# Feed forwards' inner units in three parts, one pool of 4 KB buffers, and an order of issue by traced durations

## The chip, the cores and the metric

The kernel runs on one core of a Trainium2 chip. The metric is device time in microseconds (us) of one launch, lower is better; times before are of three runs, and one more execution was profiled.

## What is computed

Two streams of 256 tokens and 1024 channels, latents (L) and context (C), pass through two layers; only the latents are returned. Shortened from the reference:

```
def ada_in(h, g, m, j):      # norm, scale, shift
    return rms_norm(h, g) * (1 + m[:, j, 1]) + m[:, j, 0]
def gated_residual(h, m, j, y, w):
    return h + w * m[:, j, 2] * y
def swiglu(x, w_in, w_out):  # 1024 -> 2 x 2816 -> 1024
    a, b = split(x @ w_in, 2); return (silu(a) * b) @ w_out

for i in range(2):           # m = silu(c) @ w_mod[i] + b_mod[i], for L and for C
    h = gated_residual(h, m, 0, swiglu(ada_in(h, g[i,0], m, 0), ...), 0.5)   # both streams
    y = retention(...) if i == 0 else neighbourhood_attention(...)
    h = gated_residual(h, m, 1, y, 1.0)
    h = gated_residual(h, m, 2, swiglu(ada_in(h, g[i,2], m, 2), ...), 0.5)
return rms_norm(h[L], final_norm_g)
```

The four feed forwards are called FFN 0 to FFN 3 here; retention stands between FFN 0 and FFN 1, attention between FFN 2 and FFN 3. Since the context isn't returned, FFN 3 and the attention's output are of the latents alone. Everything is in float32.

## The kernel before

Activations lie with channels on the 128 partitions: a stream is 8 chunks of 128 channels x 256 tokens. A product in float32 is made of three matmuls in the fp32r format: each operand is split into a high part (a cast on ScalarE, ACT) and a low part (the difference, on VectorE, DVE), and TensorE (PE) adds high x high, high x low and low x high in one bank. So each weight is loaded (`raw`), cast (`whi`) and subtracted (`wlo`) before PE can use it, and each activation too (`slot` tiles).

A feed forward (`ffn`, line 725) takes the 2816 inner units as 22 blocks of 128, in two halves of 11 (`HALF`). In each half it makes 11 gated blocks (one 1 MB weight each, two banks, 48 matmuls of both streams' 512 columns), and then adds their products with the output weights to the 8 output blocks of 128 channels: for each block n one weight of 11 x 128 columns, 33 matmuls into one bank, and one `residual` per stream, `h<-one,gate,h` on DVE. In the second half the last two output blocks (n = 6, 7) are done stream by stream: first L's two, 256 columns wide, then C's two, so that L's norm can begin while PE works on C. This norm is a chain: square (ACT), sum (DVE), sum over partitions (`rstd_rows`, two small matmuls on PE, `one<-con,t` 128x2), reciprocal root (`rsqrt`, eight small steps on DVE, `few`), diagonal (`t<-con,few`), spread over the partitions (`rstd_cols`, two matmuls `one<-t,con` 128x128), and for each of 8 chunks a scaling (`t<-h,scl,one`, DVE), a high part (ACT) and a low part (`slot<-t,modT,slot`, DVE). The next stage's first weights then run stream by stream: `pair` matmuls of 256 columns for L, later for C.

PE, DVE, ACT and GpSimd run their instructions in the order in which the program issues them; no scheduler moves them. The program sets this order by a clock of its own: each issue adds a cost to the engine's time (`account`, line 131; `Engine`, line 143; `mm`, line 258), and after each matmul `advance` (line 228) issues those steps whose time has come: norm steps (`later`), casts and subtractions of weights (`soon`), and steps of the modulation (`bg`, `acc<-mraw`: the sums of silu(c) with w_mod, one step every `BG_EVERY` us). SyncE (SP) issues the loads. Weights have buffers of their own: two `raw` of 8 KB a partition, three pairs `whi`, `wlo` of 8 KB; activations have 24 `slot` buffers of 4 KB. The costs are

```
V = Engine("dve", nc.vector, 0.06, 960.0)      # fixed us, elements per us
A_ = Engine("act", nc.scalar, 0.09, 1200.0)
account("pe", [lhsT, rhs], [out], n / 2400.0 * (1 if rhs.dtype == F32R and n >= 256 else 4) + 0.0025)
BG_EVERY = 2.2
RAWS, SPLITS = 2, 3
```

Of the kernel before, what the change touches and what calls it, by code (L numbers as in the profile page):

```python
# [17 lines left out]
P = 128  # L18
# [6 lines left out]
HALF = NHC // 2  # L25
# [4 lines left out]
H_RET = 4  # L30
BIG = 1e30

# [39 lines left out]
def trunk(ctx, tc, a):  # L72
# [4 lines left out]
    slots = ctx.enter_context(tc.tile_pool(name="slots", bufs=24))  # L77
# [83 lines left out]
    V = Engine("dve", nc.vector, 0.06, 960.0)  # L161
    A_ = Engine("act", nc.scalar, 0.09, 1200.0)
# [26 lines left out]

    plan = []  # L190

    def plan_all():
        for f in range(2):
            for hf in range(2):
                plan.extend(a["win"][f, hf * HALF + t] for t in range(HALF))
                plan.extend(a["wout"][f, hf, n] for n in range(KC))
            if f == 0:
                for hd in range(H_RET):
                    plan.extend([a["rq"][hd], a["rk"][hd], a["rv"][hd, 0], a["rv"][hd, 1]])
                    if hd:  # L200
                        plan.extend([a["ro"][hd - 1, 0], a["ro"][hd - 1, 1]])
                    plan.extend([a["rg"][hd, 0], a["rg"][hd, 1]])
                plan.extend([a["ro"][H_RET - 1, 0], a["ro"][H_RET - 1, 1]])
        for f in range(2, 4):
            for hf in range(2):
                plan.extend(a["win"][f, hf * HALF + t] for t in range(HALF))
                plan.extend(a["wout"][f, hf, n] for n in range(KC))
            if f == 2:
                for g in range(4):
                    plan.extend([a["nq"][g], a["nk"][g], a["nv"][g]])  # L210
                plan.extend(a["no"][n] for n in range(4))

    plan_all()
    RAWS, SPLITS = 2, 3
    raws, split_tiles = [], []
    state = {"loaded": 0, "freed": 0, "split": 0, "retired": 0, "bg_at": 0.0, "hold": True, "sums": True, "inside": True, "lag": (0.0, 0.0), "tight": False}
# [11 lines left out]
    def advance():  # L228
# [4 lines left out]
        while soon and not state["tight"] and soon[0][0] <= now["pe"] and ready_at(soon[0][5]) <= now["pe"] + 0.3 and free("dve", 0.5):  # L233
            soon.pop(0)[2]()
# [34 lines left out]
    def load():  # L269
# [5 lines left out]
        raws.append((t, src.shape))  # L275

    def prep():
        raw, shape = raws.pop(0)
        tile_no = state["split"]
        state["split"] += 1  # L280
        w = shape[1] * shape[2]
# [1290 lines left out]
```

## Time and profile before

| | |
|---|---|
| median of 3 runs | 1951.44 us (1949.91 to 1952.09) |
| profiled execution | 1952.25 us, span from first to last instruction 1950.2 us |
| PE busy | 1924.2 us (99%) |
| DVE busy | 1352.0 us (69%) |
| ACT busy | 687.9 us (35%) |
| loaded | 276.11 MB, 142 GB/s over the span |

Stages, in us of the span: start and FFN 0 to about 413, retention to 834, FFN 1 to 1192, FFN 2 to 1553, attention to 1746, FFN 3 and the end to 1950. "Busy" counts the time in which at least one instruction of the engine is under way; PE's matmuls overlap, so a stretch in which PE is busy throughout is one in which it never waited long enough to run empty.

### The profile page before, as it was taken

The page shows a single profiled execution, that of the slowest core. Times are in us where ns is not written, and L with a number is a line of the kernel's source. Part 1 is how long each engine was busy: PE and PEld are TensorE (multiplying, and loading weights), DVE is VectorE, ACT ScalarE, POOL GpSimd, SP SyncE. Part 2 cuts the span into 40 slices and gives each one's busy share as a digit, 9 for nine tenths or more (in the row PEclk, how much of TensorE's full clock was granted, in tenths as well). Part 3 has the DMA queues.
Part 4 walks back from the last instruction along what each step waited for, and adds up shares of the span by engine and source line. Part 5 has one row for each costly group of instructions (what it writes and reads, how often), then busy time and mean ns, then how long its engine had stood idle before and what let it go on. Part 6 is the DMA issues. An engine that isn't in the chain of part 4 may idle for free.

```text
span 1950.2 us, 26148 instructions
## 1 busy us (share of the span) xinstructions
PE 1924.2 (99%) x10458; PEld 1661.8 (85%) x10458; DVE 1352.0 (69%) x2402; ACT 687.9 (35%) x1035; POOL 73.0 (4%) x108
## 2 busy tenths in 40 slices
PE   7999999999999999999999999999999999999998
PEld 4888888898888888888888889888888899989998
DVE  5576666678788888876666676767632588887665
ACT  5422232333323232342222223322222366665443
POOL 1000000010000000100000000000000101100000
PEclk8999999999999999999999999999999999999999
DMA  7334534434434434234353343555433345544553
GB/s 287 141 137 129 187 130 136 156 119 151 142 133 141 147 130 142 86 130 149 125 179 132 140 139 98 194 189 200 162 101 82 110 119 113 98 115 167 194 176 114
DMA packets 70090, 278.85 MB, mean 143 GB/s; under 512 B 23632, under 2 KB 23888, under 8 KB 52304
## 3 DMA queue, kind: packets, MB, share of 16 engines
q1 hardware_dynamic: 69968, 277.18, 43.5%
q8 instruction: 82, 1.34, 0.3%
q14 instruction: 40, 0.33, 0.0%
HBM read 276.11 MB, written 1.05 MB: 142 GB/s over the span
## 4 chain that ended last, share of the span: by engine, by line
PE 94%; DVE 3%; ACT 2%; DMA 1%; issue 0%; SPq 0%; DVEq 0%; ACTq 0%
PE pair L259 61%; PE one L259 32%; DVE slot L151 1%; PE one L265 1%; DMA slot<-in_wmod 1%; DVE t L151 1%; ACT slot L151 1%; DVE wlo L151 1%; ACT whi L151 1%; DVE few L151 0%; DMA raw<-in_nv 0%; ACT t L151 0%; DVE h L151 0%; PE pair L265 0%; SPq L166 0%
## 5 line engine op out<-in xcount | busy, mean ns | idle before, releaser
L259 PE MATMUL pair<-slot,whi 128*128 128x512 f32 (+2 forms) x4000 | 1039.1, 351 | 6.8 <-ACT slot L151 4.7
L259 PEld LDWEIGHTS pair<-slot,whi 128*128 128x128 f32 x4000 | 696.4, 190 | 104.3 <-ACT slot L151 5.4
L259 PE MATMUL pair<-slot,wlo 128*128 128x512 f32 (+2 forms) x2000 | 682.5, 350 | 0.1
L259 PE MATMUL one<-slot,whi 128*128 128x512 f32 (+1 forms) x1860 | 481.4, 347 | 0.0
L151 DVE TENSOR_TENSOR wlo<-raw,whi 128x1024 fp32r<-128x1024 f32 (+1 forms) x400 | 436.4, 1122 | 38.5 <-ACT whi L151 37.7
L151 ACT CAST whi<-raw 128x1024 fp32r<-128x1024 f32 (+1 forms) x400 | 365.0, 959 | 225.3 <-PE one L259 138.6
L259 PEld LDWEIGHTS pair<-slot,wlo 128*128 128x128 f32 x2000 | 372.9, 190 | 48.8 <-DVE wlo L151 0.4
L259 PEld LDWEIGHTS one<-slot,whi 128*128 128x128 f32 x1860 | 325.9, 189 | 43.4
L259 PE MATMUL one<-slot,wlo 128*128 128x512 f32 (+1 forms) x930 | 323.1, 347 | 0.0
L151 DVE SCALAR_TENSOR_TENSOR acc<-mraw,sT,acc 128x512 f32<-128x512 f32 x392 | 279.2, 750 | 17.1 <-DMA mraw<-in_wmod 15.9
L151 ACT ACTIVATE t<-pair 128x512 f32<-128x512 f32 x66 | 39.4, 597 | 442.9 <-PE pair L259 442.9
L259 PEld LDWEIGHTS one<-slot,wlo 128*128 128x128 f32 x930 | 176.1, 189 | 21.8
L151 DVE TENSOR_TENSOR t<-pair,t 128x512 f32<-128x512 f32 x66 | 45.6, 692 | 204.2 <-ACT t L151 204.2
L151 DVE TENSOR_TENSOR slot<-t,slot 128x512 fp32r<-128x512 f32 (+2 forms) x144 | 88.1, 612 | 64.8 <-ACT slot L151 63.4
L151 ACT CAST slot<-t 128x512 fp32r<-128x512 f32 (+2 forms) x144 | 79.4, 552 | 122.1 <-DVE t L151 121.7
L151 DVE SCALAR_TENSOR_TENSOR h<-one,gate,h 128x256 f32<-128x256 f32 x112 | 49.6, 479 | 103.6 <-PE one L259 103.4
L151 POOL TENSOR_TENSOR t<-t,t 128x256 f32<-128x256 f32 x47 | 39.4, 850 | 1708.4 <-ACT t L151 1286.9
L259 PE MATMUL pair<-whi,slot 128*128 128x512 f32 (+1 forms) x384 | 98.5, 339 | 0.0
L259 PE MATMUL one<-slot,slot 128*128 128x512 f32 (+1 forms) x432 | 89.8, 348 | 1.3 <-DVE slot L151 1.0
L151 ACT ACTIVATE t<-h 128x256 f32<-128x256 f32 (+1 forms) x88 | 36.9, 434 | 142.8 <-DVE h L151 129.3
L259 PEld LDWEIGHTS one<-slot,slot 128*128 128x128 f32 x432 | 69.9, 189 | 10.8 <-DVE slot L151 1.4
L259 PEld LDWEIGHTS pair<-whi,slot 128*128 128x128 f32 x384 | 67.2, 189 | 7.5
(100 smaller groups left out, 1077.8 us busy)
## 6 DMA issues: line engine op xcount, KB each, us to landing
raw<-in_win SPq DMA_DIRECT2D x88, 1024.0 KB, 4.9
mraw<-in_wmod SPq DMA_DIRECT2D x128, 512.0 KB, 4.7
raw<-in_wout SPq DMA_DIRECT2D x64, 704.0 KB, 4.2
slot<-in_wmod SPq DMA_DIRECT2D x16, 512.0 KB, 10.3
raw<-in_rv SPq DMA_DIRECT2D x8, 1024.0 KB, 4.8
raw<-in_rg SPq DMA_DIRECT2D x8, 1024.0 KB, 4.9
raw<-in_ro SPq DMA_DIRECT2D x8, 1024.0 KB, 4.9
slot<-in_ex SPq DMA_DIRECT2D x8, 512.0 KB, 6.0
```

What stands on the lines that cost most here:

```text
L151: getattr(self.real, op)(*args, **kw)
L259: nc.tensor.matmul(out, lhsT=lhsT, rhs=rhs, start=start, stop=stop)
L265: nc.tensor.transpose(out=out, in_=in_, identity=ident)
```

## The change

Parts: the 22 blocks of inner units are taken in three parts of 8, 7 and 7, not in two halves of 11. So there are 96 output weights of 8 or 7 blocks instead of 64 of 11, every output block is added to `h` three times, and the last two output blocks, done stream by stream, have 7 inner blocks.

Buffers: `raw`, `whi`, `wlo` and the activations share one pool of 40 buffers of 4 KB; at most 4 hold raw weights and 12 split parts. A 1 MB weight is loaded as two halves of 512 KB.

Costs of the program's own clock: DVE and ACT get larger fixed costs, each matmul 0.0136 us on top of its columns; a background step comes every 1.6 us; `mod_sum` is held back while the values are projected; `mcol` makes the modulation's blocks that are missing.

Code for a product with 7 instead of 8 multiplications is there too (`Seven`, `seven`, `low_by_dma`), and isn't reached with `STANDARD = (22, 22, 22)`; but `operands`, which makes its inputs, is called in the third part of FFN 0, 1 and 2, and what it makes is used by nothing.

```diff
-HALF = NHC // 2
+PARTS = ((0, 8), (8, 15), (15, 22))
+SLOTS, RAWS, SPLITS = 40, 4, 12
+STANDARD, AMONG = (22, 22, 22), (2, 3, 3)
...
-    slots = ctx.enter_context(tc.tile_pool(name="slots", bufs=24))
+    slots = ctx.enter_context(tc.tile_pool(name="slots", bufs=SLOTS))
...
-    V = Engine("dve", nc.vector, 0.06, 960.0)
-    A_ = Engine("act", nc.scalar, 0.09, 1200.0)
+    V = Engine("dve", nc.vector, 0.157, 960.0)
+    A_ = Engine("act", nc.scalar, 0.155, 1150.0)
...
-        while soon and not state["tight"] and soon[0][0] <= now["pe"] and ready_at(soon[0][5]) <= now["pe"] + 0.3 and free("dve", 0.5):
+        while soon and not state["tight"] and soon[0][0] <= now["pe"] and ready_at(soon[0][5]) <= now["pe"] + 0.3 and free("dve", 0.5) and state["parts"] + soon[0][6] <= SPLITS:
...
-        account("pe", [lhsT, rhs], [out], n / 2400.0 * (1 if rhs.dtype == F32R and n >= 256 else 4) + 0.0025)
+        account("pe", [lhsT, rhs], [out], n / 2400.0 * (1 if rhs.dtype == F32R and n >= 256 else 4) + 0.0136)
...
+        for i, (raw, src) in enumerate(zip(units, srcs)):
+            n = src.shape[1] * src.shape[2]
+            hi, lo = part_tile(), part_tile()
+            def first(hi=hi, raw=raw, n=n):
+                A_.copy(out=hi[:, :n], in_=raw[:, :n])
+            def second(hi=hi, lo=lo, raw=raw, n=n):
+                V.tensor_tensor(out=lo[:, :n], in0=raw[:, :n], in1=hi[:, :n].bitcast(F32), op=ALU.subtract)
+                landed(1)
...
-    BG_EVERY = 2.2
+    BG_EVERY = 1.6
...
-        for hf in range(2):
+        for hf, (t0, t1) in enumerate(PARTS):
             gts = []
+            size, final = t1 - t0, hf == len(PARTS) - 1
...
+            if not raw and t1 == standard:
+                made_operands = operands(xt)
...
-            last = KC - 2 if hf == 1 and len(streams) == 2 else KC
+            last = KC - 2 if final and len(streams) == 2 else KC
             for n in range(2, last):
                 w, ps = weight(), one()
-                acc3(ps[:, every], terms(w, every, range(HALF)))
+                acc3(ps[:, every], terms(w, every, range(size)))
...
-                        acc3(ps[:, xc], terms(w, xc, range(HALF)))
+                        acc3(ps[:, xc], terms(w, xc, range(size)))
```

What this does to the order of issue, at three places. In the rows, the left side of the arrow is what is written; `h0` is the latents' state and `h1` the context's, `x2` means two instructions that read alike.

First, PE at the end of FFN 0, where retention begins. Before, the two spread matmuls (`one_441`) stand among the 33 matmuls of the context's last output block (`one_432`), with 29 of these behind them:

```order
L259 MATMUL one_432_3095<-slot_267_1838,whi_408_2893 128x256 x2
L259 MATMUL one_432_3095<-slot_267_1838,wlo_409_2894 128x256
L259 MATMUL one_432_3095<-slot_277_1910,whi_408_2893 128x256
L259 MATMUL one_441_3108<-t256_428_3071,con_78 128x128 x2
L259 MATMUL one_432_3095<-slot_277_1910,whi_408_2893 128x256
L259 MATMUL one_432_3095<-slot_277_1910,wlo_409_2894 128x256
L259 MATMUL one_432_3095<-slot_286_1991,whi_408_2893 128x256 x2
```

So PE had the rest of the context's block to do while DVE began the norm steps.

After, they (`one_586`) stand behind all of the context's last block (`one_562`), and the next stage's first pair (`pair_576`) directly behind them:

```order
L281 MATMUL one_562_3314<-slot_488_2885,wp_515_3047 128x256
L281 MATMUL one_562_3314<-slot_500_2970,wp_514_3046 128x256 x2
L281 MATMUL one_562_3314<-slot_500_2970,wp_515_3047 128x256
L281 MATMUL one_586_3374<-t256_566_3330,con_78 128x128 x2
L281 MATMUL pair_576_3364<-slot_578_3366,wp_531_3130 128x256
L281 MATMUL pair_576_3364<-slot_579_3367,wp_531_3130 128x256
L281 MATMUL pair_576_3364<-slot_578_3366,wp_532_3131 128x256
```

So nothing of the context stands between the spread and the pair. The row sums moved as well, from behind 17 context matmuls to behind 23 of them.

Second, DVE at the same place, from the diagonal on. Before, the context's last residual (`h1_85<-one_432`) comes amid the norm steps:

```order
L151 TENSOR_SCALAR t256_428_3071<-con_78,few_426_3061 128x128 x2
L151 SCALAR_TENSOR_TENSOR h1_85<-one_424_3039,gate_221_1443,h1_85 128x256
L151 SCALAR_TENSOR_TENSOR scl_442_3111<-modT_83,vec_80 128x8
L151 SCALAR_TENSOR_TENSOR t256_443_3116<-h0_84,scl_442_3111,one_441_3108 128x256
L151 SCALAR_TENSOR_TENSOR t256_444_3119<-h0_84,scl_442_3111,one_441_3108 128x256
L151 SCALAR_TENSOR_TENSOR slot_434_3101<-t256_443_3116,modT_83,slot_433_3100 128x256
L151 SCALAR_TENSOR_TENSOR t256_445_3133<-h0_84,scl_442_3111,one_441_3108 128x256
L151 SCALAR_TENSOR_TENSOR slot_434_3101<-t256_444_3119,modT_83,slot_433_3100 128x256
L151 SCALAR_TENSOR_TENSOR t256_446_3143<-h0_84,scl_442_3111,one_441_3108 128x256
L151 SCALAR_TENSOR_TENSOR slot_436_3103<-t256_445_3133,modT_83,slot_435_3102 128x256
L151 SCALAR_TENSOR_TENSOR h1_85<-one_432_3095,gate_221_1443,h1_85 128x256
```

Six norm steps stood ahead of that residual.

After, it and the sum of the context's squares stand between the diagonal and the first norm step:

```order
L161 TENSOR_SCALAR t256_566_3330<-con_78,few_564_3320 128x128 x2
L161 SCALAR_TENSOR_TENSOR h1_85<-one_562_3314,gate_233_1270,h1_85 128x256
L161 TENSOR_TENSOR t256_513_3041<-t256_571_3358,t256_513_3041 128x256
L161 SCALAR_TENSOR_TENSOR scl_587_3378<-modT_83,vec_80 128x8
L161 SCALAR_TENSOR_TENSOR t256_588_3380<-h0_84,scl_587_3378,one_586_3374 128x256
L161 SCALAR_TENSOR_TENSOR t256_589_3383<-h0_84,scl_587_3378,one_586_3374 128x256
L161 SCALAR_TENSOR_TENSOR slot_579_3367<-t256_588_3380,modT_83,slot_578_3366 128x256
```

The first norm step (`t256_588`) moved behind two steps that wait for the context's end.

At the ends of FFN 1 and FFN 2 the two orders differ in the same way, with one of the unused subtractions and two of weights' in the stretch besides.

Third, DVE where FFN 1 begins, in the context's norm. Before, two subtractions of weights (`wlo`) stand between the diagonal and the first norm step:

```order
L151 TENSOR_SCALAR t256_971_6679<-con_78,few_969_6669 128x128 x2
L151 TENSOR_TENSOR wlo_946_6522<-raw_883_6127,whi_945_6521 128x1024
L151 SCALAR_TENSOR_TENSOR scl_973_6706<-modT_83,vec_80 128x8
L151 TENSOR_TENSOR wlo_946_6522<-raw_883_6127,whi_945_6521 128x1024
L151 SCALAR_TENSOR_TENSOR t256_975_6723<-h1_85,scl_973_6706,one_972_6703 128x256
L151 SCALAR_TENSOR_TENSOR t256_976_6729<-h1_85,scl_973_6706,one_972_6703 128x256
L151 SCALAR_TENSOR_TENSOR slot_934_6490<-t256_975_6723,modT_83,slot_933_6489 128x256
L151 SCALAR_TENSOR_TENSOR t256_977_6741<-h1_85,scl_973_6706,one_972_6703 128x256
L151 SCALAR_TENSOR_TENSOR slot_934_6490<-t256_976_6729,modT_83,slot_933_6489 128x256
```

From the first norm step on nothing came between the steps for a while.

After, two stand ahead of the small steps, and two more (`wp`, as these parts are named now) between the first low part and the third scaling:

```order
L161 TENSOR_SCALAR t256_1196_7012<-con_78,few_1194_7002 128x128 x2
L161 SCALAR_TENSOR_TENSOR scl_1198_7044<-modT_83,vec_80 128x8
L161 SCALAR_TENSOR_TENSOR t256_1199_7049<-h1_85,scl_1198_7044,one_1197_7041 128x256
L161 SCALAR_TENSOR_TENSOR t256_1200_7052<-h1_85,scl_1198_7044,one_1197_7041 128x256
L161 SCALAR_TENSOR_TENSOR slot_1153_6801<-t256_1199_7049,modT_83,slot_1152_6800 128x256
L161 TENSOR_TENSOR wp_1179_6906<-raw_1127_6621,wp_1178_6905 128x1024
L161 TENSOR_TENSOR wp_1181_6908<-raw_1128_6623,wp_1180_6907 128x1024
L161 SCALAR_TENSOR_TENSOR t256_1203_7086<-h1_85,scl_1198_7044,one_1197_7041 128x256
L161 SCALAR_TENSOR_TENSOR slot_1153_6801<-t256_1200_7052,modT_83,slot_1152_6800 128x256
L161 SCALAR_TENSOR_TENSOR t256_1204_7092<-h1_85,scl_1198_7044,one_1197_7041 128x256
L161 SCALAR_TENSOR_TENSOR slot_1155_6803<-t256_1203_7086,modT_83,slot_1154_6802 128x256
```

So the second low part (`slot_1153` from `t256_1200`) moved behind two subtractions.

## Rows read from the trace of the kernel before

**Rows 1.** The page, busy time of each engine, share of the span, instructions.

```profile
PE 1924.2 (99%) x10458; PEld 1661.8 (85%) x10458; DVE 1352.0 (69%) x2402; ACT 687.9 (35%) x1035; POOL 73.0 (4%) x108
```

**Rows 2.** Windows: length; busy time (instructions) of PE, PEld, DVE, ACT, POOL; granted clock; DMA.

```profile
413.70:800.00 386.30, 386.30 (x1859) 325.69 (x1858) 318.86 (x581) 123.20 (x157) 0.00 (x0) 1.00 0.41 138
1727.00:1755.00 28.00, 24.02 (x183) 22.17 (x182) 23.43 (x61) 17.80 (x40) 1.62 (x2) 1.00 0.34 114
```

**Rows 3.** Groups of instructions by form: count, busy us, mean ns of one, idle before.

```profile
L151 DVE TENSOR_TENSOR wlo<-raw,whi 128x1024 fp32r<-128x1024 f32 x272 | 324.3, 1222 | 21.5 <-ACT whi L151 21.0
...
L151 DVE TENSOR_TENSOR slot<-t,slot 128x512 fp32r<-128x512 f32 x98 | 67.8, 692 | 56.8 <-ACT slot L151 56.3
...
L151 DVE SCALAR_TENSOR_TENSOR h<-one,gate,h 128x256 f32<-128x256 f32 x112 | 49.6, 479 | 103.6 <-PE one L259 103.4
```

**Rows 4.** Timeline of PE, FFN 0 to retention: start, us, line, operation.

```profile
404.70 0.40 PE L259 MATMUL one<-slot,whi 128*128 128x256 f32 x2
...
406.74 0.51 PE L259 MATMUL one<-con,t 128*128 128x2 f32 x4
...
409.58 0.60 PE L259 MATMUL one<-t,con 128*128 128x128 f32 x4
...
413.49 0.40 PE L259 MATMUL pair<-slot,whi 128*128 128x256 f32 x2
...
419.69 1.36 PE L259 MATMUL pair<-slot,whi 128*128 128x256 f32 x10
```

**Rows 5.** Timeline of DVE, the same stretch.

```profile
404.90 0.48 DVE L151 SCALAR_TENSOR_TENSOR h<-one,gate,h 128x256 f32<-128x256 f32 x1 [2.34 <-PE one L259]
...
407.28 0.16 DVE L151 TENSOR_SCALAR few<-one 128x2 int32<-128x2 int32 x1 [0.86 <-PE one L259]
...
409.30 0.48 DVE L151 SCALAR_TENSOR_TENSOR h<-one,gate,h 128x256 f32<-128x256 f32 x1
...
410.22 0.87 DVE L151 SCALAR_TENSOR_TENSOR t<-h,scl,one 128x256 f32<-128x256 f32 x2 [0.36 <-PE one L259]
411.28 0.48 DVE L151 SCALAR_TENSOR_TENSOR slot<-t,modT,slot 128x256 fp32r<-128x256 f32 x1 [0.19 <-ACT slot L151]
...
413.70 0.49 DVE L151 SCALAR_TENSOR_TENSOR h<-one,gate,h 128x256 f32<-128x256 f32 x1 [0.35 <-PE one L259]
...
414.88 0.42 DVE L151 TENSOR_TENSOR t<-t,t 128x256 f32<-128x256 f32 x1
...
417.85 0.48 DVE L151 SCALAR_TENSOR_TENSOR slot<-t,modT,slot 128x256 fp32r<-128x256 f32 x1 [0.18 <-ACT slot L151]
```

**Rows 6.** Timeline of PE, retention to FFN 1.

```profile
833.84 0.60 PE L259 MATMUL one<-t,con 128*128 128x128 f32 x4
...
838.83 0.40 PE L259 MATMUL pair<-slot,whi 128*128 128x256 f32 x2
```

**Rows 7.** Timeline of PE, end of the attention; in brackets the idle time before.

```profile
1735.75 0.63 PE L265 MATMUL one<-con,t 128*128 128x128 f32 x4 [0.52 <-DVE t L151]
...
1737.06 0.74 PE L259 MATMUL one<-slot,slot 128*128 128x256 f32 x4 [0.32 <-ACT slot L151]
1738.32 0.74 PE L259 MATMUL one<-slot,slot 128*128 128x256 f32 x4 [0.52 <-DVE slot L151]
...
1741.81 0.84 PE L259 MATMUL pair<-slot,whi 128*128 128x256 f32 x2 [1.33 <-ACT slot L151]
```

**Rows 8.** The page, DMA issues: count, KB each, us from issue to landing.

```profile
mraw<-in_wmod SPq DMA_DIRECT2D x128, 512.0 KB, 4.7
```

**Rows 9.** Windows of the start, columns as in rows 2.

```profile
24.00:28.00 4.00, 2.33 (x11) 1.67 (x12) 3.45 (x11) 2.53 (x6) 0.00 (x0) 0.92 1.01 406
28.00:30.00 2.00, 1.93 (x9) 1.64 (x9) 2.00 (x4) 2.00 (x4) 0.00 (x0) 0.50 1.02 408
38.00:40.00 2.00, 1.29 (x4) 1.06 (x5) 1.82 (x6) 1.31 (x3) 0.00 (x0) 0.50 0.05 18
44.00:46.00 2.00, 2.00 (x12) 1.91 (x11) 2.00 (x3) 2.00 (x3) 0.00 (x0) 0.50 0.00 0
```

More of the change, by code (lines that the diff above doesn't have):

```diff
@@ L213, in trunk @@
     plan_all()
-    RAWS, SPLITS = 2, 3
-    raws, split_tiles = [], []
-    state = {"loaded": 0, "freed": 0, "split": 0, "retired": 0, "bg_at": 0.0, "hold": True, "sums": True, "inside": True, "lag": (0.0, 0.0), "tight": False}
+    raws, split_tiles, active = [], [], []
+    state = {"loaded": 0, "raw": 0, "split": 0, "parts": 0, "limit": SPLITS, "bg_at": 0.0, "hold": True, "sums": True, "inside": True, "lag": (0.0, 0.0), "tight": False}
     soon = []
@@ L300, in pump, with released @@
+    def released(n):
+        state["parts"] -= n
+        pump()
     def pump():
         while True:
-            if raws and state["split"] - state["retired"] < SPLITS:
+            if raws and (not split_tiles if raws[0][0] == "seven" else
+                         state["parts"] + 2 * len(raws[0][1]) <= state["limit"] and not any(x[6] for x in soon)):
                 prep()
-            elif state["loaded"] < len(plan) and state["loaded"] - state["freed"] < RAWS:
+            elif state["loaded"] < len(plan) and state["raw"] + len(plan[state["loaded"]][1]) <= RAWS:
@@ L446, in mcol @@
         c0 = (j * 3 + w) * KC
-        assert all((l, v, (c0 + k) // 4) in made for k in range(kk.start, kk.stop))
+        while not all((l, v, (c0 + k) // 4) in made for k in range(kk.start, kk.stop)):
+            if due:
+                mod_sum(*due.pop(0)[1])
+            else:
+                next(bg, None)
         return modT[:, l, v, c0 + kk.start:c0 + kk.stop]
@@ L782, in ffn @@
                 state["hold"] = False
-            for t in range(len(gts), HALF):
+            for t in range(len(gts), size):
+                if t0 + t == standard:
+                    x7 = made_operands()
+                    state["limit"] = SPLITS
+                if in_seven(2 * l + which, t0 + t):
+                    gts.append(slot([P, 2, 512], F32R))
+                    seven(t, gts[t], x7)
+                    continue
+                if not raw and t0 + t == standard - 3 and standard < PARTS[0][1]:
+                    made_operands = operands(xt)
+                if t0 + t == standard - 3 and standard == PARTS[0][1]:
+                    state["limit"] = SPLITS - 4
                 wh, wl = weight()
```

288 lines of the change are left out of this document (231 added, 57 removed).

## The prediction, made before the changed kernel ran

> **What bounds the kernel now.** I read the page's table of engines first: TensorE (PE) is busy 1924.2 of 1950.2 us, VectorE (DVE) 1352.0 [rows 1]. A PE row counts as busy while its pipeline drains, so 99% does not say that PE runs at its peak; but it says that PE hardly ever waits. The windows say where it does: not at all from 413.70 to 800.00, which is all of retention but its end, and 3.98 us (28.00 - 24.02) at the end of the attention [rows 2]. The remaining idle PE time is the start and the last 8 us, which the change leaves as they are (the first 130 instructions of PE's order read the same in both kernels).
>
> So two things can move the time: the number and width of the matmuls, and new waits of PE. Everything that DVE and ACT do is free until PE arrives at an instruction whose operand isn't there. The places where this is decided are those where one stage's output must pass a chain of small steps before the next stage's first matmul: residual, square, sum, reciprocal root, spread over the columns, scaled and split.
>
> That chain as it runs now, from FFN 0 to retention: PE has finished the latents' last two output blocks and starts on the context's at 404.70. DVE adds the last residual (404.90), ACT squares, PE sums rows at 406.74, eight small steps and the diagonal run on DVE from 407.28 to 409.30, PE spreads the result at 409.58, the first norm step is at 410.22, the last low part is written from 417.85 to 418.33 [rows 4, 5]. Beside it PE does 66 context matmuls of 256 columns. Their pitch is 0.120 us (seventeen stand ahead of the row sums, from 404.70 to 406.74), so they are 7.92 us of cover. PE starts the next stage's first pair at 413.49, and 404.70 + 7.92 + 0.37 (rows) + 0.36 (spread) = 413.35: no wait. The low part of the eighth chunk is ready at 418.33, and PE asks for it at about 413.49 + 42 x 0.120 = 418.5 or a little after. So this chain fits with next to nothing to spare.
>
> **The change part by part.**
>
> *Matmuls.* The last two output blocks are done stream by stream in 256 columns, and now have 7 inner units instead of 11. By the two orders there are 144 matmuls of 256 columns less and 72 of 512 columns more. At 0.120 us for the narrow ones, and between 0.213 (512 columns at the granted 2.4 GHz; the clock is 1.00 in [rows 2]) and 0.240 (twice a narrow one) for the wide ones, this is -1.9 to 0 us. I take **-0.9**.
>
> *Cover of the three chains: FFN 0 to retention, FFN 1 to FFN 2, FFN 2 to attention.* The same 7 for 11 takes the context's cover from 66 to 42 matmuls, 5.04 us. The order shows two things more: the row sums now stand 23 matmuls behind the latents' end (before: 17), and on DVE the last context residual and its sum stand ahead of the first norm step, not amid the norm steps. Counted from the context's first matmul, after, by the durations of before:
> - row sums at 23 x 0.120 = 2.76; small steps 0.54 behind them (406.74 to 407.28), but not before the first context residual, so 3.4; diagonal done 2.02 later (407.28 to 409.30), 5.4;
> - the last context matmul ends its issue at 5.04 + 0.37 = 5.41, so its residual starts at about 5.65, and its sum 1.18 later (413.70 to 414.88), 6.83; the first norm step behind both, 7.25 (before: 410.22 - 404.70 = 5.52);
> - from the first norm step to the end of the last low part it takes 418.33 - 410.22 = 8.11 now, with a residual and a sum amid it that use up 0.40 and 0.34; without them 7.37. So the last low part is there at 14.6;
> - PE needs it some 0.7 us before the end of the first weight's latent part: 15.3. Before, this end was at 419.69 - 404.70 = 15.0, with 24 x 0.120 = 2.88 us more work in it.
>
> The loss is 15.3 - (15.0 - 2.88) = 3.2 us for each, **+9.6** for three. Bounds: if the residual and its sum do not delay the first norm step, it is 7.25 - 5.52 = 1.7 less each (1.5, in all 4.5); if the weights' subtractions, 1.22 us [rows 3], that stand in the chain at the second and third place are in the way once each, 12.0.
>
> *Retention to FFN 1.* The cover is the same, but DVE's order is not. Now the spread stands at 833.84 and the context's first pair at 838.83 [rows 6], 5.0 us. After, only 13 matmuls (1.56 us) stand between spread and pair, and two subtractions stand behind the first low part. From the spread to the first low part it takes 2.18 us (409.58 to 411.28 + 0.48 [rows 4, 5]), so PE, which comes 1.56 + 0.36 behind it, waits 0.3. The second low part comes two subtractions (2.3), a norm step and itself (0.4 + 0.4) later, at 5.3; PE wants it 12 matmuls after the first, at 3.7: 1.6 more. With some 0.4 for a later spread, **+2.3** (0 if the subtractions were done early, 3 if all of it shows).
>
> *End of the attention.* The four waits ahead of the last head's products and its share of the output projection sum to 0.52 + 0.32 + 0.52 + 1.33 = 2.69 us [rows 7]. In the order of after 18 + 24 = 42 projection matmuls stand between that head's last product and the first matmul that needs its result, not 12. That is 30 x 0.120 = 3.6 us of cover more, which takes the wait of 1.33 away and may take part of the others: **-2.0** (0 to -2.7).
>
> *Costed at nothing.* (a) 56 more residuals of 0.479 us are 26.8 us of DVE; the unused operands that are still built after each of the first three feed forwards are 24 sums of 128x512 (0.692 each) and 24 operations of 128x1024 (1.222 each), 46 us of DVE [rows 3], and 12 casts on ACT. DVE is idle for 598 us [rows 1] and PE goes ahead meanwhile; if this cover were gone in the 386 us stretch, where DVE is at 318.86 [rows 2], there would be 67 us left. Only the steps within the chains above count, and they are in the sums. (b) The pieces in which weights are loaded are half as large, and PE's first use of one stands at least 26 us of matmuls behind its load in the order, where the least was 12; a load of that size lands in 4.7 us [rows 8]. (c) The background steps come every 1.6 us, not 2.2, but they are as many: they are done earlier, out of retention and FFN 2 into the stages before.
>
> *Sum:* 9.6 + 2.3 - 0.9 - 2.0 = +9.0. The profiled execution took 1952.25 us, 0.8 over the median of 1951.44. So 1960.4 against the median, **1960.5**.
>
> **The rivals.**
>
> *The clock falls too.* A wait of 3 us may cost more than itself. At the start, PE was busy only 2.33 of 4.00 us from 24 to 28, and its granted clock was 0.50 (1.2 GHz) in the next 2 us; after a second thin stretch it was at 0.50 from 38 to 46, though PE was busy all of the last 2 us ([rows 9]; of the four rows from 38 to 46, which all have 0.50, the first and the last stand there). It did not fall at the attention's end, where the idle time came in pieces of at most 1.33 us (clock 1.00 [rows 2]). At half clock a stretch of 3 to 8 us loses 1.5 to 4 us, for each of three waits: +5 to +12 if all fall, so **1967** (1964 to 1973). For it: the wait of about 3 us in one piece. Against it: the four waits of the attention's end, which followed closely, did not do it. [...]
>
> *The waits close up (no change).* The chain runs tighter because nothing interrupts it, and the first norm step comes at 5.5, not 7.25; the weights' subtractions are done ahead. Then 4.5 + 0 - 0.9 - 2.0 = +1.6, or +0.9 with the attention's end in full: **1952.5**. For it: DVE still idles 0.36, 0.19 and 0.35 us between steps of the chain [rows 5], which could close. Against it: the residual follows PE's end within 0.2 us (413.49 to 413.70 [rows 4, 5]) and can't come sooner, and in the new order all of the chain stands behind it.
>
> *The new order wins.* One mechanism: the three chains stay covered, because the row sums and the spread are reached by PE as soon as DVE has them, and the attention's end loses all of its 2.69. Then -0.9 - 2.7 = **1948**. It decides where the last low part comes less than 11 us behind the context's first matmul (5.04 + 0.73 + 5.04); now it comes 418.33 - 404.70 = 13.6 us behind it [rows 4, 5].
>
> *DVE is too full in FFN 0* (residuals, background and unused sums at once) and PE waits for weights: 67 us of slack would have to go, so it is unlikely; some 10 us on top, 1970.
>
> **How the numbers follow.** Chances: forecast 0.50, clock 0.14, no change 0.18, new order wins 0.14, DVE 0.04. About 0.2% (3.9 us) is what a measurement of this kernel can tell from no change. The forecast's own range is 1955 to 1965; of its half I count 0.03 as below 1955.3. Slower: 0.47 + 0.14 + 0.04 = 0.65; same: 0.18 + 0.03 = 0.21; faster: 0.14. The range reaches from 1950 (leaving out about a tenth, the wins) to 1968 (leaving out the worse half of the clock's case and DVE's).
>
> **What would show it.** Right: PE idle 2.5 to 4 us just behind the spread at each of the three transitions, released by the first low parts, with DVE busy without a gap from the first norm step to the last; about 2 us idle behind the retention's spread; the 1.33 us at the attention's end gone; no wait of PE on a weight's part anywhere else. Wrong: PE without a gap at the transitions, or a granted clock below 1.00 behind them, or PE waiting for weights' parts inside a feed forward.

## The result, and the profile after

The changed kernel took 1973.66 us (median of 4 runs, 1971.30 to 1974.95), the kernel before 1951.74 in the same runs: a ratio of 1.0113, 95% interval 1.0095 to 1.0130. It is slower, as forecast, but by 21.9 us and not by 9, and outside the range given.

The page of the changed kernel, beside [rows 1]: 72 matmuls less and yet 7.5 us more of busy PE, most of it likely matmuls at a lower clock (at most 7.0 us, as worked out below); DVE has 69.4 us more.

```profile
PE 1931.7 (98%) x10386; PEld 1664.5 (84%) x10386; DVE 1421.4 (72%) x2474; ACT 695.7 (35%) x1015; POOL 86.1 (4%) x108
```

Now its windows around the five places where one stage hands over to the next, in the columns of [rows 2]: the end of FFN 0, retention to FFN 1, FFN 1 to FFN 2, FFN 2 to attention, attention to FFN 3.

```profile
400.00:430.00 30.00, 26.84 (x188) 25.26 (x187) 26.09 (x58) 13.86 (x23) 8.06 (x7) 0.94 0.22 70
820.00:860.00 40.00, 38.57 (x317) 37.77 (x315) 27.94 (x72) 16.39 (x32) 5.42 (x8) 1.00 0.17 54
1190.00:1220.00 30.00, 26.36 (x209) 25.54 (x208) 26.27 (x62) 12.98 (x23) 4.93 (x6) 1.00 0.21 71
1555.00:1595.00 40.00, 36.06 (x254) 34.59 (x253) 33.77 (x74) 16.95 (x30) 10.89 (x10) 0.91 0.33 105
1730.00:1770.00 40.00, 37.65 (x285) 35.50 (x284) 34.13 (x73) 28.45 (x60) 5.33 (x6) 0.96 0.62 193
```

Length less PE's busy time is its idle time: 3.16, 1.43, 3.64, 3.94 and 2.35 us. In the kernel before, the first and the fifth of these places read:

```profile
400.00:430.00 30.00, 30.00 (x254) 30.00 (x253) 23.05 (x64) 12.64 (x25) 1.81 (x2) 1.00 0.21 71
1720.00:1760.00 40.00, 36.02 (x282) 34.04 (x281) 32.25 (x76) 24.30 (x53) 3.09 (x4) 1.00 0.29 103
```

So before, PE idles 0.00 us at each of the first three places, 0.06 at the fourth (1545 to 1585) and 3.98 at the fifth (40.00 - 36.02, in a window of 40 us that holds all of the 28 us in [rows 2]). The second thing to see is the granted clock, 0.94, 0.91 and 0.96 where it was 1.00: for part of these windows it was 0.50. There one matmul of 256 columns follows the other every 0.213 us (in the rows from 419.93 and from 1570.89), at 1.00 every 0.120. So such a stretch loses 0.44 of its length, and (1 - clock) x length, which counts half of it, bounds what that cost: 1.8, 3.6 and 1.6 us.

The sum, against before: idle time 3.16 + 1.43 + 3.64 + 3.88 - 1.63 = 10.5; clock at most 7.0; another 0.92 us in FFN 0, where PE waits for the modulation's sums at 149.83 (shown below); -0.9 for the matmuls: 17.5 of the span's 20.4 us. Of the rest 1.5 us is idle time elsewhere, 0.7 of it in the first 60 us (in all PE idles 38.9 us of the span, and 26.0 before). The last 1.4 us may lie in the first 0.16 us of each of some ten waits, in which the last matmul's row still counts as busy: a row of 256 columns lasts 0.28 us, and the next starts 0.120 behind it (from 404.94 in the kernel before). That is an estimate; no row shows it.

The first transition, row by row. PE of the changed kernel, start, us, operation, in brackets the idle time before and who ended it:

```profile
408.39 4.00 PE L281 MATMUL one<-slot,wp 128*128 128x256 f32 x32
412.49 0.61 PE L281 MATMUL one<-con,t 128*128 128x2 f32 x4
...
416.27 0.71 PE L281 MATMUL one<-t,con 128*128 128x128 f32 x4 [0.80 <-DVE t L161]
419.11 1.24 PE L281 MATMUL pair<-slot,wp 128*128 128x256 f32 x3 [2.13 <-ACT slot L161]
```

Of the 32 matmuls at 408.39 the first 9 are the latents', so the context's work starts at 408.39 + 9 x 0.120 = 409.47, where [rows 4] had 404.70. DVE of the same stretch:

```profile
409.24 1.76 DVE L161 TENSOR_TENSOR wp<-raw,wp 128x1024 fp32r<-128x1024 f32 x1
410.92 0.47 DVE L161 SCALAR_TENSOR_TENSOR h<-one,gate,h 128x256 f32<-128x256 f32 x1
...
412.35 1.22 DVE L161 TENSOR_TENSOR wp<-raw,wp 128x1024 fp32r<-128x1024 f32 x1
...
413.88 0.15 DVE L161 TENSOR_SCALAR few<-one 128x2 int32<-128x2 int32 x1
...
416.32 0.48 DVE L161 SCALAR_TENSOR_TENSOR h<-one,gate,h 128x256 f32<-128x256 f32 x1
417.42 0.43 DVE L161 TENSOR_TENSOR t<-t,t 128x256 f32<-128x256 f32 x1 [0.61 <-ACT t L161]
...
418.03 0.87 DVE L161 SCALAR_TENSOR_TENSOR t<-h,scl,one 128x256 f32<-128x256 f32 x2
...
424.49 0.48 DVE L161 SCALAR_TENSOR_TENSOR slot<-t,modT,slot 128x256 fp32r<-128x256 f32 x1 [0.18 <-ACT slot L161]
```

The latents' last residual starts at 410.92, 1.45 us behind the context's first matmul, not 0.20 as at 404.90 in [rows 5]: a subtraction of a weight stands ahead of it and takes 1.76 us, not 1.22 [rows 3]. A second one, at 412.35, stands ahead of the small steps. From there all is later than I had put it: small steps at 4.4 us (3.4), residual and sum of the context in the order shown with the change, first norm step at 418.03, that is 8.6 (7.25), last low part done at 424.97, 15.5 (14.6).

Then the clock. The same stretch in windows of 2 us:

```profile
414.00:416.00 2.00, 1.47 (x13) 1.26 (x11) 1.72 (x9) 0.42 (x1) 0.74 (x1) 1.00 0.55 139
416.00:418.00 2.00, 0.71 (x4) 0.52 (x4) 1.31 (x5) 0.42 (x1) 0.00 (x0) 1.00 0.92 365
418.00:420.00 2.00, 0.75 (x3) 0.56 (x4) 1.78 (x5) 0.91 (x2) 0.00 (x0) 0.94 0.08 29
420.00:422.00 2.00, 2.00 (x11) 2.00 (x11) 2.00 (x6) 1.44 (x3) 0.00 (x0) 0.50 0.00 0
422.00:424.00 2.00, 2.00 (x15) 2.00 (x14) 2.00 (x6) 1.16 (x4) 0.00 (x0) 0.71 0.00 0
```

PE is busy 1.47, 0.71 and 0.75 of 2 us, and then runs without a gap at 0.50 and 0.71: the low parts that it waited for are there, and it works at the clock of 0.50 for some 3 us, with a matmul every 0.213 us.

What a transition costs in all can be measured as the prediction reckoned it, from the context's first matmul to the end of the first weight's latent part (the start of the 49th matmul of the pair). At the three places this takes 17.8, 16.9 and 19.3 us in the change, and 15.0, 15.0 and 15.5 before with 2.88 us more work in it. So the losses are 5.7, 4.8 and 6.6 us, 17.2 in all. The last low part is there 15.5, 15.7 and 17.5 us behind the context's first matmul.

The waits of 0.9 us and more at the other places, in the order of time, from PE's timelines: the modulation's sums; retention to FFN 1; FFN 1 to FFN 2 (sum of rows, first pair); FFN 2 to attention (the same two); FFN 3's start.

```profile
149.83 0.41 PE L281 MATMUL one<-small,con 128*128 128x32 f32 x2 [0.92 <-DVE small L161]
...
849.81 1.45 PE L281 MATMUL pair<-slot,wp 128*128 128x256 f32 x10 [1.36 <-DVE slot L161]
...
1199.44 0.58 PE L281 MATMUL one<-con,t 128*128 128x2 f32 x4 [0.90 <-DVE t L161]
...
1205.80 1.38 PE L281 MATMUL pair<-slot,wp 128*128 128x256 f32 x6 [2.60 <-ACT slot L161]
...
1569.05 0.58 PE L281 MATMUL one<-con,t 128*128 128x2 f32 x4 [1.48 <-DVE t L161]
...
1576.68 3.66 PE L281 MATMUL pair<-slot,wp 128*128 128x256 f32 x14 [2.37 <-ACT slot L161]
...
1763.41 2.12 PE L281 MATMUL pair<-slot,wp 128*128 128x256 f32 x12 [1.70 <-DVE h L161]
```

From FFN 2 to attention the clock falls to 0.50 twice. The second time is behind the 2.37 us (0.50 from 1577 to 1580), the first behind the wait of 1.48 us ahead of the row sums, while PE still works on the context's matmuls, and so the context's last residual and the chain behind it come later too:

```profile
1571.00:1573.00 2.00, 2.00 (x11) 2.00 (x11) 1.28 (x6) 0.42 (x1) 0.03 (x1) 0.50 0.46 186
```

### The profile page after: what moved, and what is told of

Its sections match the earlier page's. It is cut to its first block, busy times and chain, and to the rows that moved or that the text cites. A ratio compares the mean times of both kernels' runs of the same rounds, so it can differ in the third digit from the quotient of the medians.

```text
span 1970.6 us, 26566 instructions
## 1 busy us (share of the span) xinstructions
PE 1931.7 (98%) x10386; PEld 1664.5 (84%) x10386; DVE 1421.4 (72%) x2474; ACT 695.7 (35%) x1015; POOL 86.1 (4%) x108
## 3 DMA queue, kind: packets, MB, share of 16 engines
q8 instruction: 81, 1.33, 0.3%
## 4 chain that ended last, share of the span: by engine, by line
PE 91%; DVE 5%; DMA 1%; ACT 1%; issue 1%; SPq 0%; DVEq 0%; POOL 0%; ACTq 0%
PE pair L281 61%; PE one L281 29%; DVE slot L161 1%; DVE wp L161 1%; PE one L287 1%; DMA slot<-in_wmod 1%; DVE t L161 1%; DVE h L161 1%; ACT slot L161 1%; DMA raw<-in_no 1%; DVE few L161 0%; ACT t L161 0%; ACT wp L161 0%; DVE acc L161 0%; SPq L176 0%
## 5 line engine op out<-in xcount | busy, mean ns | idle before, releaser
L281 PE MATMUL pair<-slot,wp 128*128 128x512 f32 (+2 forms) x6000 | 1151.6, 352 | 15.9 <-ACT slot L161 10.4
L281 PEld LDWEIGHTS pair<-slot,wp 128*128 128x128 f32 x6000 | 981.0, 191 | 163.5 <-ACT slot L161 12.3
L281 PE MATMUL one<-slot,wp 128*128 128x512 f32 (+1 forms) x2718 | 522.0, 353 | 0.0
L281 PEld LDWEIGHTS one<-slot,wp 128*128 128x128 f32 x2718 | 446.6, 190 | 67.9
L161 DVE TENSOR_TENSOR wp<-raw,wp 128x1024 fp32r<-128x1024 f32 (+1 forms) x368 | 432.4, 1209 | 24.3 <-ACT wp L161 21.7
L161 ACT CAST wp<-raw 128x1024 fp32r<-128x1024 f32 (+1 forms) x368 | 360.8, 1026 | 128.0 <-DMA raw<-in_win 69.5
L281 PE MATMUL pair<-wp,slot 128*128 128x512 f32 (+1 forms) x576 | 104.5, 338 | 1.4 <-DVE slot L161 1.4
L281 PEld LDWEIGHTS pair<-wp,slot 128*128 128x128 f32 x576 | 89.6, 189 | 13.1 <-DVE slot L161 1.9
L161 ACT ACTIVATE slot<-t,modT 128x256 fp32r<-128x256 f32 x80 | 39.4, 507 | 55.5 <-DVE t L161 55.5
L161 DVE TENSOR_TENSOR slot<-slot,slot 128x512 f32<-128x512 f32 (+2 forms) x52 | 53.3, 1060 | 6.5 <-ACT slot L161 6.4
```

Source lines behind the costliest of these rows:

```text
L161: getattr(self.real, op)(*args, **kw)
L281: nc.tensor.matmul(out, lhsT=lhsT, rhs=rhs, start=start, stop=stop)
```

## The experiments

After the result my theory was "cover": 7 inner units in the last part leave too little context work beside the norm chain, and the clock falls on top. The rivals: "DVE" (unused operations and subtractions stretch the chain) and "order" (the program's new costs put steps in the wrong places). Ratios are to the kernel before in the same runs, with 95% intervals.

**1. More cover.** In `ffn`, three output blocks stream by stream:

```diff
-            last = KC - 2 if final and len(streams) == 2 else KC
+            tail = 3
+            last = KC - tail if final and len(streams) == 2 else KC
...
-                ws = [weight(), weight()]
+                ws = [weight() for _ in range(tail)]
...
```

> The changed kernel, but the last three output blocks (not two) of FFN 0 to 2 are done stream by stream, so that 63 context matmuls (7.56 us) instead of 42 (5.04) lie beside the latents' norm chain; it costs 21 matmuls of 512 columns turned into 42 of 256 (0.3 us) in each. Theory 'cover' (the three transitions lose because the chain is longer than the context work beside it, and the clock falls on top): PE's wait behind the spread shrinks by about 2.5 us at each and the clock stays at 1.00 there, in all 8 to 12 us back, 1962 to 1966. Rival 'DVE' (unused operations and weight subtractions stretch the chain, cover does not matter): no more than 2 us back, since the same steps stand in the chain.

1968.86 us, 1.0086 (1.0071 to 1.0101): 4.8 us back, half of what "cover" said. PE's idle time in windows at the three transitions fell from 10.7 to 6.5 us (1.91, 2.33, 2.21), but the clock still showed 0.94 and 0.96 at the second and third.

**2. Without the unused operands.**

```diff
-            if not raw and t1 == standard:
-                made_operands = operands(xt)
```

> The changed kernel without the unused operands (46 us of DVE and 12 casts of ACT less; the output does not depend on them). Theory 'cover': one stretched step less in each chain, 1 to 3 us back, 1971 to 1973. Rival 'DVE': most of the loss at the three transitions goes, 10 us or more back, 1964 or less.

1969.54 us, 1.0094 (1.0079 to 1.0109): 4.1 us back, a little more than "cover" said and far from what "DVE" said (the intervals of this ratio and of the change's overlap, so the 4 us are not sharp). The idle time at the transitions stayed at 10.2 us (4.51, 2.28, 3.39).

**3. The old costs, parts and pool as changed.**

```diff
-    V = Engine("dve", nc.vector, 0.157, 960.0)
-    A_ = Engine("act", nc.scalar, 0.155, 1150.0)
+    V = Engine("dve", nc.vector, 0.06, 960.0)
+    A_ = Engine("act", nc.scalar, 0.09, 1200.0)
...
-else 4) + 0.0136)
+else 4) + 0.0025)
...
-    BG_EVERY = 1.6
+    BG_EVERY = 2.2
```

> The changed kernel with the old costs of the program's own clock (DVE 0.06, ACT 0.09 and 1200, 0.0025 per matmul, a background step every 2.2 us); parts and pool as changed. Theory 'cover': the three transitions still lose, 1966 to 1974. Rival 'order' (the new costs put the context's last residual and the spread in the wrong places): the first norm step comes again amid the context's work, back to 1951 to 1957.

1974.47 us, 1.0122 (1.0107 to 1.0137): the same as the change, so the costs are not what makes the parts slow. Its windows show it more sharply, in part because this execution, the profiled one, took 1978.53 us at a mean granted clock of 0.986, where the other three took 1974.08 to 1974.62 at 0.989:

```profile
405.00:435.00 30.00, 25.26 (x158) 24.13 (x158) 24.97 (x55) 12.92 (x22) 8.03 (x6) 0.77 0.27 88
820.00:860.00 40.00, 40.00 (x335) 39.91 (x335) 32.25 (x78) 19.28 (x37) 7.51 (x10) 1.00 0.28 95
1195.00:1225.00 30.00, 27.45 (x194) 26.45 (x193) 23.05 (x60) 11.38 (x22) 6.19 (x6) 0.89 0.32 106
1565.00:1605.00 40.00, 36.47 (x252) 35.15 (x251) 30.38 (x74) 17.02 (x31) 8.47 (x8) 0.87 0.29 94
```

The three transitions idle 4.74, 2.55 and 3.53 us and fall to a clock of 0.77 to 0.89, but retention to FFN 1 (820 to 860) has no idle time at all. That wait is of the new costs. A fourth loss is new in this run: with a background step every 2.2 us PE waits 3.57 us for the modulation's sums in FFN 0, at 151.45, and the clock falls to 0.50 behind it. In the change that wait is 0.92 us, likely thanks to its faster background.

**4. The parts alone, in the kernel before** (its own buffers and costs; `PARTS` for `HALF` in the plan and in `ffn`, and missing blocks of the modulation are made when asked for, as in the change).

> The kernel before with the three parts alone (its own buffers, costs and order rules; no unused operands). Theory 'cover': the transitions lose some 3 us each and the clock may fall, 1958 to 1966. Rivals 'order' and 'DVE': no loss, 1949 to 1953.

1979.71 us, 1.0145 (1.0128 to 1.0162): slower than the whole change, and more than any theory said. Beside the transitions PE waits for a weight's low part at 393.62 (2.50 us), for the modulation's sums at 150.73 (1.85 us), and FFN 3 (1820 to 1910) idles 2.24 us. Of this 1.78 us stand at 1900 to 1903, where a gated block's weight is cast and subtracted too late; ACT's cast of it, at 1900.13, had waited 2.71 us for PE, likely for one of the three pairs of 8 KB buffers, of which the smaller output weights fill one each. "No loss" of the rivals is out.

**5. The new costs alone, in the kernel before** (the edit of run 3 the other way round).

> The kernel before (halves of 11, its own buffers) with the new costs of the program's own clock and a background step every 1.6 us; nothing else. Theory 'cover': no transition loses, since 66 context matmuls lie beside the chain; 1948 to 1953. Rival 'order' (the new costs themselves put steps in the wrong places): PE waits at the transitions, 1955 or more.

1963.79 us, 1.0068 (1.0053 to 1.0083). My theory had 1948 to 1953 and was wrong; the rival "order" was right about this. PE idles 2.87 us at the end of FFN 0 (1.4 of it for the modulation's sums), 1.17 behind retention, 1.31 behind FFN 1, 4.68 at the attention's end and FFN 3's start (1720 to 1775).

**6, 7. Both: more cover and no unused operands**, with three and with four blocks stream by stream (the edits of runs 1 and 2; `tail = 4`).

> The changed kernel with both: three output blocks done stream by stream, and no unused operands. On record here as the joint theory: chain and cover both count, and the one hid the other's worth in the two runs that changed one alone. By its order the row sums stand behind 17 context matmuls and 20 stand behind the spread, as before the change. Joint theory: under 1 us of wait at each transition, clock 1.00, 1957 to 1961. If only cover counts: as the first run with three blocks, 1967 to 1969.

1966.04 us, 1.0078 (1.0063 to 1.0093): slower than the joint theory said and faster than "only cover"; 2.94, 1.49 and 1.26 us idle, clock 1.00 at all three. Two things stand against the joint theory. At FFN 3's start, which this edit leaves alone, the clock fell to 0.50 (at most 3.6 us in the window 1730 to 1770). And at the first transition PE waits 1.68 us ahead of the row sums, at 410.53, because on DVE two subtractions of weights stand ahead of the latents' last two residuals, which start at 408.17:

```profile
405.81 2.44 DVE L161 TENSOR_TENSOR wp<-raw,wp 128x1024 fp32r<-128x1024 f32 x2 [1.09 <-ACT wp L161]
```

> As the run before with four output blocks stream by stream (84 context matmuls, 10.08 us of cover): joint theory: no wait at the transitions, but 21 matmuls of 512 columns more in pairs of 256 in each feed forward (0.3 us each): 1955 to 1960. If the weights' subtractions that the longer tail pushes back decide, a new wait on weights' parts and 1962 or more.

1963.63 us, 1.0065 (1.0050 to 1.0080), 3.6 us above the upper bound and in the range of the expectation's second branch (1962 or more). But the second and third transition are clean now. The first keeps 1.73 us of idle time (3.16 in the change) and the clock of 0.94; it is one wait ahead of the row sums, at 408.04, again with two subtractions amid the latents' last residuals:

```profile
400.00:430.00 30.00, 28.27 (x225) 28.07 (x224) 21.32 (x55) 11.06 (x21) 5.78 (x7) 0.94 0.44 148
820.00:860.00 40.00, 38.57 (x317) 37.95 (x316) 27.60 (x72) 16.36 (x31) 5.84 (x8) 1.00 0.01 2
1190.00:1220.00 30.00, 30.00 (x251) 29.71 (x249) 22.01 (x59) 11.99 (x22) 3.01 (x4) 1.00 0.13 42
1555.00:1595.00 40.00, 40.00 (x337) 40.00 (x336) 29.30 (x73) 20.25 (x36) 5.17 (x7) 1.00 0.28 85
1730.00:1770.00 40.00, 37.57 (x302) 36.17 (x301) 32.51 (x78) 25.45 (x54) 3.88 (x4) 1.00 0.55 186
```

So at the second and third transition enough cover does take the waits away, and the clock's fall with them; at the first it does not, with 84 context matmuls beside the chain. What else remains is retention to FFN 1, FFN 3's start, the modulation, and single waits of up to 1.6 us within retention and the attention.

**8. Parts of 7, 7 and 8** with three blocks and no unused operands.

> As the run with three blocks and no unused operands, but parts of 7, 7 and 8, so that 72 context matmuls (8.64 us) lie beside the chain, and the first gates are needed a little earlier. Joint theory: waits at the transitions below 0.5 us, and a longer wait for the modulation in FFN 0 by up to 1 us: 1956 to 1960.

1972.19 us, 1.0110 (1.0093 to 1.0127): a miss. PE's waits behind the spread are 0.52, 0.52 and 2.04 us, so the third is not below the 0.5 hoped for; the clock is 1.00 at all three. But the first gates are needed some 12 us sooner, and PE waits 7.46 us for the modulation's sums at 143.65, where the change waits 0.92, and the clock falls behind it (0.75 over 130 to 150, at most 5 us). Smaller first parts pull the background's due time forward.

**9. The parts undone**, everything else as changed but for the operands. So that an output weight of 11 blocks fits the buffers, it comes in pieces of 6 and 5:

```diff
-PARTS = ((0, 8), (8, 15), (15, 22))
+PARTS = ((0, 11), (11, 22))
...
-            plan.extend(("plain", [a["wout"][f, n][:, t0:t1, :]]) for n in range(KC))
+            plan.extend(("plain", [a["wout"][f, n][:, t0:t0 + 6, :], a["wout"][f, n][:, t0 + 6:t1, :]]) for n in range(KC))
```

> The changed kernel with the parts undone: two halves of 11 again (an output weight comes as pieces of 6 and 5 blocks, so that it fits the 4 KB buffers), no unused operands; pool and new costs as changed. Theory 'cover' (the parts cause the waits at the transitions, with 7 blocks beside the chain): PE waits under 1 us at each transition, clock 1.00, some 16 us less than the changed kernel, 1955 to 1959; what stays is the retention to FFN 1 wait and the new wait at FFN 3's start, which I put to the costs. Rival (the costs cause most of it, as the run with the costs alone, 1963.8, suggests): 1962 or more.

1958.81 us, 1.0036 (1.0022 to 1.0049), as "cover" said. Its windows:

```profile
400.00:430.00 30.00, 29.66 (x245) 29.23 (x245) 21.30 (x57) 11.55 (x21) 1.47 (x2) 1.00 0.40 136
820.00:860.00 40.00, 37.94 (x289) 36.22 (x288) 28.71 (x64) 19.73 (x35) 3.70 (x5) 1.00 0.01 3
1190.00:1220.00 30.00, 29.44 (x242) 28.81 (x241) 22.73 (x61) 12.44 (x22) 0.73 (x1) 1.00 0.38 124
1550.00:1590.00 40.00, 39.35 (x328) 39.11 (x327) 29.30 (x72) 19.46 (x34) 2.87 (x4) 1.00 0.35 112
1720.00:1760.00 40.00, 36.73 (x290) 34.86 (x289) 34.13 (x80) 26.43 (x58) 4.60 (x5) 1.00 0.62 188
```

0.34, 0.56 and 0.65 us at the three transitions, clock 1.00; idle time at retention to FFN 1 is still there (2.06 us). The cover is 66 context matmuls, nearly the 63 of run 6, and yet 1.55 us are idle at the three places where run 6 has 5.69. At the first place DVE is idle ahead of the latents' last residual in this run, so no subtraction holds up the chain's start:

```profile
404.94 0.48 DVE L161 SCALAR_TENSOR_TENSOR h<-one,gate,h 128x256 f32<-128x256 f32 x1 [2.73 <-PE one L281]
```

**10. The pool alone**: run 9 with the old costs of run 3. What is left of the change is the pool and the code around it, `mod_sum` held back among it.

> As the run before, with the old costs and a background step every 2.2 us: the pool alone. Theory 'cover' with costs as the second cause: nothing waits that did not wait before, 1949 to 1953. If the pool or the loads of 512 KB and less cost by themselves: 1955 or more.

1949.68 us (10 runs), 1951.79 before; 0.9989 (0.9980 to 0.9999): a little faster than the kernel before and the fastest of all. Nothing waits at the first four places:

```profile
400.00:430.00 30.00, 30.00 (x254) 30.00 (x253) 22.36 (x62) 11.81 (x24) 1.48 (x2) 1.00 0.38 127
820.00:860.00 40.00, 40.00 (x297) 38.19 (x296) 32.30 (x67) 20.03 (x34) 3.81 (x5) 1.00 0.16 54
1190.00:1220.00 30.00, 30.00 (x236) 29.21 (x236) 22.61 (x52) 14.94 (x26) 0.00 (x0) 1.00 0.35 107
1550.00:1590.00 40.00, 39.94 (x330) 39.56 (x329) 33.57 (x76) 23.49 (x39) 2.32 (x3) 1.00 0.43 134
1720.00:1750.00 30.00, 27.32 (x214) 25.75 (x214) 25.43 (x61) 19.82 (x46) 3.11 (x4) 1.00 0.51 167
```

**11. The new costs of DVE, ACT and matmul in the kernel before, the background's rate as before.**

> The kernel before with the new costs of DVE, ACT and matmul, but a background step every 2.2 us as before. The run with all of the new costs lost 12.9 us: if the background's rate is the cause (its waits on a weight's low part and on the modulation's sums in FFN 0, 373 to 401 us), 5 us or more come back and 1955 to 1959; if the costs of the engines are, it stays at 1961 to 1966.

1958.31 us, 1.0035 (1.0022 to 1.0047): 5.5 us come back from run 5, as the first branch said. The rate of the background is nearly half of what the costs lose there.

**12. The matmul's new cost alone**, on the pool of run 10 (`+ 0.0136` for `+ 0.0025`).

> The pool with halves and the old costs (the run that took 1949.7), with the matmul's new cost alone (0.0136 us on top of its columns). With all the new costs it took 1958.8. If the larger fixed costs of DVE and ACT are what makes the program issue norm steps and subtractions too late, this stays at 1948 to 1951, without a wait of 1.5 us behind the retention and without one of 1.85 us at FFN 3's start; if the matmul's cost is, 1955 to 1959 with these waits.

1958.92 us, 1.0038 (1.0023 to 1.0052). My guess that the engines' costs are to blame fell as to the time, and held as to one place:

```profile
820.00:860.00 40.00, 40.00 (x317) 39.08 (x317) 30.09 (x76) 18.87 (x35) 3.93 (x5) 1.00 0.17 54
1600.00:1760.00 160.00, 154.33 (x1090) 141.78 (x1089) 129.87 (x266) 100.78 (x196) 23.46 (x31) 1.00 0.58 121
```

No wait behind retention, so that one is of DVE's and ACT's costs or of the background's rate, both of which are the old ones here. In the old buffers this place idles 1.17 us with all new costs (run 5) and 0.56 with the background as before (run 11), so likely both have a part in it. But with the matmul's cost alone PE idles 5.67 us in the attention and at FFN 3's start (run 10 has 2.69 in the same window), and it waits 3.00 us for a weight's low part at 377.92 in FFN 0, with a clock of 0.85 over 376 to 380. The two costs lose their time in different places and do not add up: 9 us with the one, and 9 with both and the background (run 9).

## Why the prediction was wrong in size

Step by step of the change, from runs that differ in one thing, by their ratios to the kernel before: pool and the code around it -2 us (run 10), new costs +9 (10 to 9), parts +11 (9 to 2), unused operands +4 (2 to the change). With the old costs the parts and the operands together are +26 (10 to 3), part of which is the wait of 3.57 us for the modulation's sums and the clock's fall behind it. So the parts are the largest item in either order, as forecast, and what each item costs depends on the others.

**Matmuls, -0.9**: right as to the count, PE has 10386 matmuls for 10458; the gain is too small to be seen by itself. No run shows a wide one at the 0.213 us of the lower bound: at clock 1.00 one follows the other every 0.227 us (39 of them in the kernel before, from 859.91 to 868.75), and 72 x 0.227 - 144 x 0.120 = -0.9. What the forecast calls 2.4 and 1.2 GHz the rows show as columns: 256 more of them take 0.227 - 0.120 = 0.107 us at 1.00, 2.4 per ns, and 256 take 0.213 us at 0.50, 1.2 per ns.

**Cover of the three chains, +9.6: the step that failed.** Measured as the forecast reckoned it, this term is 17.2 us (5.7, 4.8 and 6.6), above even its bound of 12.0. The mechanism is right in part: halves in place of parts (run 9) leave 1.6 us of run 2's 10.2 us of idle time, and a tail of four blocks (run 7) leaves 1.7. But cover is not all of it, as runs 6 and 9 show (nearly the same cover, 5.69 and 1.55 us idle): the chain also begins later, behind subtractions of weights. No run moved these subtractions alone.

The size was off twice. First, the chain: I placed each step by the durations of before, and let subtractions of weights count only in the bound, one each at the second and third place and none at the first. At the first place two stood there, one ahead of the latents' last residual, stretched to 1.76 us, and one ahead of the small steps. The last low part, worked out at 14.6, came at 15.5, 15.7 and 17.5 (at the second and third place the row sums stood behind 20 context matmuls, not 23, and yet PE waited 0.90 and 1.48 us ahead of them). So PE waits 7.1 us (2.13 + 2.60 + 2.37) behind the spread, where I had 9.6, and 3.2 us (0.80 + 0.90 + 1.48) ahead of it, where I had nothing. That the idle time in all, 10.7 us, is close to 9.6 is partly luck.

Second, the clock, which this sum has at nothing: at most 5.4 us at the first and third transition. I had it as a rival of its own, at 0.14 and 1967, "for each of three waits", and named a clock below 1.00 as a sign of being wrong. It fell at two of the three and at FFN 3's start, and came on top of a later chain, so that 1973.66 lies above even that rival's 1973. My argument against it, that four close waits did not lower the clock, did not reach this case: those waits were 0.3 to 1.33 us long, and the waits behind which it fell here 1.48 to 2.37.

**Retention to FFN 1, +2.3**: 1.43 us idle, 1.36 of it ahead of the second low part as forecast; mechanism and place right. Runs 3, 9 and 12 show whose it is: of the new costs (of DVE, ACT or the background), not of the parts.

**End of the attention, -2.0: wrong.** All four waits of [rows 7] are gone, the 1.33 us ahead of the output projection with them, but FFN 3's start waits 1.70 us for DVE's state in their place and the clock falls there: 2.35 idle + 1.6 for 3.98 before, which is no gain. I followed the fill that the order moved behind the last head, and did not ask what then came last.

**Costed at nothing.** The operands cost 4 us (run 2), most of it not at the transitions, where only 0.6 us of idle time came back; where the rest was lost I did not follow. The background, done earlier, was still not early enough: with parts the first gates are due sooner, and PE waits 0.92 us in the change, 7.46 in run 8, 3.57 at the old rate (run 3). No weight's part was late in the change itself, as forecast; the pool is the likely reason, since the parts without it waited (run 4) in FFN 0 and FFN 3.

**The rivals.** "The waits close up" and "the new order wins" needed the chain to be shorter; it was longer. "DVE is too full" was wrong as to weights. The idle time that I put down to start and end alone had some 2 us more elsewhere before the change, too little to matter here.

What stays open: why costs closer to the traced durations make a worse order. Runs 5, 9, 11 and 12 show that they do, at which places, and that the effects do not add; they don't show a rule. A reading that I have not tested is that steps issued too early only wait on an engine that has room, while steps issued just in time by the program's clock come late on the chip.

## What to carry to other kernels

When the size of a part changes, count the instructions that lie beside each serial chain at the hand-over, and place everything that stands ahead of the chain on its engine at full length, not in a bound. A wait of TensorE can have two prices, itself and the half clock behind it (here behind waits of 1.48 to 2.37 us, but not behind one of 2.60); cost them together. And undo one part of a bundle at a time: here one of three, the common pool with the code around it, was a small gain (0.9989) that the others hid.

## What the hardware showed that I had not expected

The clock did not fall at every wait of this length: behind the wait of 2.60 us at 1205.80, with 0.90 us idle 6 us earlier, the granted clock stayed at 1.00, and behind 2.13 and 2.37 us at the other two it fell to 0.50. The total idle time in the windows is nearly the same (3.16, 3.64, 3.94).

FFN 3's start shows the same with one and the same wait. In the change and in runs 1, 2, 6, 7, 8 and 9 PE waits 1.69 or 1.70 us there for the latents' state. Behind it the clock fell to 0.50 in the change and in runs 2 and 6, and stayed at 1.00 in runs 1, 7, 8 and 9. The same 34 matmuls, in run 6 and then in run 7:

```profile
1758.51 6.93 PE L281 MATMUL pair<-slot,wp 128*128 128x258 f32 x34 [0.67 <-DVE h L161]
1757.50 4.34 PE L281 MATMUL pair<-slot,wp 128*128 128x258 f32 x34 [0.74 <-DVE h L161]
```

So an estimate can't tell from the length of a wait alone whether the clock falls behind it, and up to 3.6 us between two runs such as 6 and 7 can be that alone.

DVE's subtraction of 1.22 us took 1.76 us while GpSimd added squares. The timeline of GpSimd has its three additions in one row, at 409.24 to 411.0 beside the subtraction:

```profile
407.30 4.30 POOL L161 TENSOR_TENSOR t<-t,t 128x256 f32<-128x256 f32 x3 [3.27 <-ACT t L161]
```

1.43 us each, where 32 others of its operations on the same shape take 0.78. In the kernel before, a row of two such additions from 398.13 overlapped a subtraction at 399.34 by little, and that took 1.30. The next subtraction, at 401.34, began ahead of an addition at 402.08: it kept its 1.22 us, and the addition took 1.07. So in these rows the one that begins second takes longer, and a subtraction beside an addition is not lengthened each time (the one at 406.96 in the change took 1.21 too). No run here took the additions away, so what they cost in all was not measured.
